# A two-layer hybrid decoder trunk: a root on ScalarE in the last norm, a decay table in two loads, keys copied by ScalarE, and the order of the first and last MLP groups

## The chip, the cores and the metric

One Trainium2 chip, one core of it. The time is device microseconds of one execution of the whole program: inputs in HBM, output in HBM. The median of three executions of the kernel before is 808.08 us (807.40 to 808.43).

## The reference

The input is 256 tokens of 1024 channels in float32. Two layers each do a mixer and an MLP, and a last RMSNorm follows. Cut to what the change touches:

```python
def rms_norm(x, g, eps=1e-6):
    return x * lax.rsqrt(jnp.mean(x * x, axis=-1, keepdims=True) + eps) * g

for l in range(2):
    h = rms_norm(x, attn_norm[l])
    p = h @ w_in[l]      # split into cq, ckv, k_rope, mq, mk, mv, rq, rk, rv, rg and three gates
    o_mla  = mla_branch(cq, ckv, k_rope, ...)       # norms of cq and ckv, up-projections, rope, causal softmax, 8 heads
    o_moba = moba_branch(mq, mk, mv, ...)           # causal softmax, 8 heads
    o_ret  = retention_branch(rq, rk, rv, rg, ...)  # rope, scores times a decay table, group norm, 4 heads
    merged = (sigmoid(g_mla) * (o_mla @ w_branch_mla) + sigmoid(g_moba) * (o_moba @ w_branch_moba)
              + sigmoid(g_ret) * (o_ret @ w_branch_ret))
    x = x + merged @ w_out[l]
    h = rms_norm(x, mlp_norm[l])
    x = x + jnp.square(jax.nn.relu(h @ w_up[l])) @ w_down[l]     # 1024 -> 4096 -> 1024
return rms_norm(x, final_norm)
```

## The kernel before, in words

**Precision.** Float32 products are made of three matmuls of split operands. A weight block arrives by DMA as `raw` (128x1024), ScalarE (ACT) rounds it to `whi` (L281), VectorE (DVE) subtracts to make `wlo` (L283), and `three` (L301) issues high by high, high by low and low by high into one PSUM bank (L302 to L304). Activations are split in the same way, as `xs` in the projections and as `sq` in the MLP's second product. In the projections whose output is wanted turned (`project_turned`, L506: keys and queries), the activations' two halves lie side by side, so that `acc` has two halves, and `join` (L493) adds them: ACT copies the second half (`second`), DVE adds it to the first (`qkraw`), and only then is the bank free for another product.

**Order of the work.** Each layer walks through units in this order: `b0` (the MLA's compressed columns c, and the first norm's sums), `mq`, `mk`, the MLA's up-projections `qrope`, `qnope` and `kvup`, `mv`, the gates, the retention's `rqk`, `rv` and `rg`, the branch products, `wout`, then the MLP in eight groups of 512 hidden columns. Steps that belong to no unit are hung into a slot of one with `at(slot(key, j), step)`. The order on each engine is then set by the tile framework's scheduler, except where the code pins it: `tc.keep_in_program_order`, `tc.issue_after`, and the table `behind`, which names for a weight block the instructions that its fetch, with its rounding, must come after (`have`, L203). Weight blocks are fetched in a fixed list, six pairs of rounded blocks deep.

**Copies of c (L819).** `c_copies` takes c out of PSUM in layer 1 and squares it; it is hung at the first unit of `mq`. `c_norms` follows a unit later.

**Keys of the MLA (L969, L1000).** `nope` copies the four 64x512 pieces of the keys out of PSUM into `KK`, and `kvup` calls it with DVE's copy; the same function copies the queries `Q` with ACT. The scores (L1039) read both.

**Retention tables (L1051).** `load_dec` loads one 1 MB table `dec` on SP's queue at the second unit of `rqk`. Its last 512 columns are the rope table, which DVE scales into `tab` (L526); its first 1536 are the decay, which the retention scores read (L1113). The rope multiplies `qkraw` and its swapped copy `qkoth` by parts of `tab` (L1097) and adds them (L1098); `swapped` (L531) makes `qkoth` with four DMAs on SP. `omlal` is the low half of the MLA's output.

**MLP (L1310 to L1372).** For each group, `squared_relu` takes two banks out with relu, squares them on ACT, and `turned_blocks` (L334) transposes them in 32x32 blocks on DVE, writes them to HBM (`bounce`) and reads them back in four DMAs (`hturned`), which turns them. `split_turned` rounds them to `sq` on ACT and subtracts on DVE (both L323). Some groups use a seven-product scheme in which sums of weight halves are made on DVE (`tsums`, `wsum`, L240) and rounded on ACT (`thi`, L233). In the last group, the weight fetches of the next blocks run on.

**Last norm (L1564 to L1587).** For each of two row tiles: ACT squares each of two 512-column banks with an accumulated sum (`fsq`, L1565), DVE adds the sums, POOL raises to the power -1/2 (L1580), DVE multiplies each bank by the gain out of PSUM (L1581), and the row factor is then applied by ACT to columns 0 to 319 and by DVE to the other 704 (L1583, L1586), each with its own output DMA.

Of the kernel before, what the change touches and what calls it, by code (L numbers as in the profile page):

```python
# [7 lines left out]
F32 = mybir.dt.float32  # L8
F32R = mybir.dt.float32r
BF16 = mybir.dt.bfloat16  # L10
AF = mybir.ActivationFunctionType
ALU = mybir.AluOpType
AX = mybir.AxisListType

P = 128
D = 1024
# [3 lines left out]
KD = D // P  # L20
DFF = 4096
NF = DFF // P
# [7 lines left out]
EPS = 1e-6  # L30
# [113 lines left out]
K_DEC = K_TURNED_MLA + 2 * S  # L144
K_TURNED_RT = K_DEC + RT_H * 3 * P
K_TURNED_MB = K_TURNED_RT + 2 * S
# [10 lines left out]
def trunk(ctx: ExitStack, tc: tile.TileContext, gx, wts, consts, gfin, gn, xtok, out):  # L157


    nc = tc.nc  # L160
# [4 lines left out]
    sb = ctx.enter_context(tc.tile_pool(name="sb", bufs=1))  # L165
# [10 lines left out]
    K = cp.tile([P, K_DEC], F32, name="K")  # L176
# [7 lines left out]
    neghalf = cp.tile([P, 8], F32, name="neghalf")  # L184
# [7 lines left out]
    order, loaded = list(where), {}  # L192
# [8 lines left out]
    behind = {}  # L201
# [110 lines left out]
    def small(name):  # L312
        return sb.tile([P, 8], F32, name=name, tag="st", bufs=SMALL)
# [20 lines left out]
    def turned_blocks(rows, name, tag, bufs, last=None, then=()):  # L334

        blocks = blocks_tile(name)
        for t in range(NT):
            turn = turn_row(blocks, t, rows[t])
        for key in then:
            behind.setdefault(key, []).append(turn)  # L340
        return turned_by_hbm(blocks, name, tag, bufs, last)
# [456 lines left out]
    def at(slot, step):  # L798
        steps.setdefault(slot, []).append(step)

    def slot(key, j):
        return [k for k, _ in prog].index((key, j))
# [9 lines left out]
    def layer(l, xn, before):  # L812

        c0 = []
        c, mla, mqkv, rqkv = {}, {}, {}, {}

        b0 = []

        def c_copies():  # L819

            for t in range(NT):
                ct = w2k("c0")
                m = small("ssc")
                c0.append((ct, m))
                nc.scalar.activation(ct[:, :416], b0[t][:, :416], AF.Copy)  # L825
                junk = sb.tile([P, 3 * P], F32, name="junk", tag="prob", bufs=4)
                for i, cs in enumerate((slice(0, MLA_QR), slice(MLA_QR, MLA_QR + MLA_KVR))):
                    n = cs.stop - cs.start
                    nc.scalar.activation(junk[:, :n], ct[:, cs], AF.Square, scale=n**-0.5, accum_out=m[:, i : i + 1])
# [98 lines left out]
        if l:  # L928
            project_turned(l, "mq", xn, moba_pair("mq"))
            for n in range(KD):  # L930
                at(slot("b0", 7), lambda n=n: xn.square(n))
            at(slot("mq", 0), c_copies)
            at(slot("mq", 1), c_norms)
            at(slot("mq", 2), xn.stats_row)
        else:
            mq = []
            for k in range(KD):
                prog.append((("start", k), lambda k=k: start(k, mq)))
            at(slot("start", KD - 2), lambda: xn.stats_rows(xrows))
            at(slot("start", KD - 1), c_copies)  # L940
            at(slot("start", KD - 1), c_norms)
            at(slot("start", KD - 1), xn.stats_row)
        project_turned(l, "mk", xn, moba_pair("mk"))
# [25 lines left out]
        def nope(dst, w, ks, copy, bank):  # L969
            for b in range(2):  # L970
                acc = bank("nope")
                for i in range(2):
                    cs = slice(P * (2 * b + i), P * (2 * b + i) + P)
                    for j, k in enumerate(ks):
                        three(
                            acc[:, S * i : S * i + S], w[0][:, j, cs], w[1][:, j, cs], c["h"][:, k, :], c["l"][:, k, :],
                            j == 0, j == len(ks) - 1,
                        )
                copy(dst[0:64, 4 * b : 4 * b + 4 : 2, :], halves(acc)[0:64])
                copy(dst[64:P, 4 * b + 1 : 4 * b + 4 : 2, :], halves(acc)[64:P])  # L980
# [18 lines left out]

        def kvup():  # L1000
            wh, wl = load_w(l, "kvup", 0)
            nope(mla["K"], (wh[:, :, 0:512], wl[:, :, 0:512]), (2,), nc.vector.tensor_copy, misc_tile)
            for t in range(NT):
                acc = misc_tile("pv")
                sl = slice(P * t, P * t + P)
                three(acc, c["h"][:, 2, sl], c["l"][:, 2, sl], wh[:, 0, 512:1024], wl[:, 0, 512:1024], True, True)
                nc.scalar.activation(mla["v"][t], acc, AF.Copy)
# [40 lines left out]

        th_moba = gates(l, "gmoba", xn)

        def load_dec():  # L1051

            rqkv["dec"] = sb.tile([P, K_TURNED_MB - K_DEC], F32, name="dec", tag="Q", bufs=1)
            tc.keep_in_program_order(nc.sync.dma_start(rqkv["dec"], consts[:, K_DEC:K_TURNED_MB]))

        merged, mT = {}, []
        if l == 0:
# [135 lines left out]
            tc.keep_in_program_order(nc.sync.dma_start(rg["gn"], src))  # L1193

        project(l, "rg", xn, 512, rg_done)
        at(slot("rqk", 1), load_dec)
        at(slot("rg", 2), load_gn)
        th_ret = gates(l, "gret", xn)
        order_out = ExitStack()
# [108 lines left out]
        us, h2, latest = {}, {}, []  # L1308
# [25 lines left out]
        def squared_relu(g):  # L1334

            rows = [w2k("relu") for _ in range(NT)]
            for t in range(NT):
                relu = nc.scalar.activation(rows[t], us[g][t], AF.Relu, scale=xm.col[t])
            for t in range(NT):
                nc.scalar.activation(rows[t], rows[t], AF.Square)  # L1340
            if g:
                waiting[g] = turned_blocks(rows, "h", "t4", T4)
            else:
                waiting[g] = turned_blocks(rows, "h", "t4", T4, (l, "down", 4, 0), [(l, "down", 2, 0)])
            if SEVEN[l][0] <= g - 2 < NF // 4 - 3:
                behind.setdefault(order[3 if g - 2 in SEVEN[l] else 4], []).append(relu)
            if 1 < g < NF // 4 - 1:
                h_ready(g - 1, relu)
            elif g != 1:
                h_ready(g)  # L1350
# [169 lines left out]
        if not last:  # L1520
            xn = Normed(G_ATT + KD * (l + 1), KD - 2)
            ys = {}


            have(ENDS[l])
            for j in range(ENDS[l], 4):
                behind[l + 1, "b0", j] = latest
            have(4)

            def copied(q):  # L1530
                ys[q] = w2k("ydn")
                copy = nc.vector.tensor_add(ys[q], accs[q], share[q])
                if q == 0:
                    tc.keep_in_program_order(copy)

            def turned(q):
                t, half = quarters[q]
                pt = misc_tile("pyd")
                for i in range(4):
                    nc.tensor.transpose(pt[:, P * i : P * i + P], ys[q][:, P * i : P * i + P], ident)  # L1540
                x_t = X[half][:, :, P * t : P * t + P]
                add = nc.vector.tensor_add(x_t, x_t, pt.rearrange("p (k s) -> p k s", k=4))
                if q == 0:
                    tc.keep_in_program_order(add)
                return xn.take_part(t, half)

            for q in range(4):
                ends[q]()
                copied(q)
                if q:  # L1550
                    turned(q - 1)

            def before(i):
                if i == 2:
                    behind[l + 1, "mq", 0, 0] = turned(3)
                if i == 7:
                    order_pe.close()

            return xn, before
# [7 lines left out]
        for t in range(NT):  # L1567
            y = sb.tile([P, D], F32, name="y", tag="t4", bufs=T4)
            r = sb.tile([P, 1], F32, name="fr", tag="st", bufs=SMALL)
            s0, s1, s2 = (st[:, 3 * t + i : 3 * t + i + 1] for i in range(3))  # L1570
            for half in range(2):
                cs = slice(512 * half, 512 * half + 512)
                ends[2 * t + half]()
                acc = accs[2 * t + half]
                if t == 0:
                    x_add(t, half)
                square(acc, 3 * t + half)
                if half:
                    nc.vector.scalar_tensor_tensor(s2, s0, EPS, s1, op0=ALU.add, op1=ALU.add)
                    nc.gpsimd.tensor_tensor(r, s2, neghalf[:, 0:1], op=ALU.pow)  # L1580
                nc.vector.tensor_mul(y[:, cs], acc, gf[:, cs])  # L1581
            cs = slice(0, 320)
            nc.scalar.activation(y[:, cs], y[:, cs], AF.Copy, scale=r)  # L1583
            nc.scalar.dma_start(out[:, t, cs], y[:, cs])
            cs = slice(320, D)
            nc.vector.tensor_scalar(y[:, cs], y[:, cs], r, None, op0=ALU.mult)  # L1586
            nc.sync.dma_start(out[:, t, cs], y[:, cs])  # L1587
        order_pe.close()
        return None, None

# [112 lines left out]
```

## Time and profile before

| what | value |
|---|---|
| median of three runs | 808.08 us |
| the profiled execution, and its span | 807.2 us, 805.4 us |
| granted TensorE clock, mean | 0.998 of 2.4 GHz |
| TensorE (PE) busy, matmuls | 797.0 us (99%), 3915 |
| DVE, ACT, POOL busy | 675.8 us, 483.1 us, 73.2 us |
| moved by DMA | 192.11 MB, 239 GB/s |
| chain that ended last | PE 89%, DMA 5%, DVE 3%, ACT 1% |

A span is from the first to the last instruction of the profiled execution; the execution's own time lies 1.8 us above it. Start times in rows count from the start of the span. In a timeline row the first number is the start, the second the duration in us (of the whole row where it stands for several, xN), then engine, line, operation, output and input; a bracket at the end gives the idle time before it and what ended it. PE is TensorE's matmul, SPq the DMA issue of the queue.

### The profile page before, as it was taken

How to read it: one execution, taken by the hardware profiler on the slowest of the kernel's cores; microseconds unless marked ns; L12 is line 12 of the kernel's file. 1: busy time of each engine (PE TensorE's matmuls, PEld its weight loads, DVE VectorE, ACT ScalarE, POOL GpSimd, SP SyncE). 2: the span in 40 equal slices, each digit the busy share in tenths (PEclk: the TensorE clock that was granted, in tenths of full speed). 3: DMA queues.
4: the chain of work that ended last, by engine and by line, in shares of the span. 5: the costliest groups of instructions: out<-in, count | busy, mean ns of one | idle time of the engine just before them, and what ended most of it. 6: DMA issues, size and time to landing. Idle time of an engine off the chain costs nothing.

```text
span 805.4 us, 11403 instructions
## 1 busy us (share of the span) xinstructions
PE 797.0 (99%) x3915; PEld 665.1 (83%) x3915; DVE 675.8 (84%) x1136; ACT 483.1 (60%) x747; POOL 73.2 (9%) x63
## 2 busy tenths in 40 slices
PE   9999999999999999999999999999999999999996
PEld 7888887888888888888788888888888878888885
DVE  6769997978888898887797987699698878899786
ACT  7775654653557666666486566655545666667562
POOL 0100810000030000000025220000000300000000
PEclk9999999999999999999999999999999999999999
DMA  9975889975678677778656579688665687788741
GB/s 335 338 244 179 281 241 297 282 235 173 222 225 244 228 255 248 252 269 259 209 163 228 157 232 326 213 261 273 217 223 192 186 272 260 241 280 319 261 169 54
DMA packets 68122, 192.11 MB, mean 239 GB/s; under 512 B 8288, under 2 KB 25056, under 8 KB 67808
## 3 DMA queue, kind: packets, MB, share of 16 engines
q1 hardware_dynamic: 67488, 190.71, 72.4%
q8 instruction: 31, 0.51, 0.3%
q10 hardware_dynamic: 576, 0.67, 0.2%
q14 instruction: 27, 0.22, 0.1%
HBM read 168.81 MB, written 18.87 MB: 233 GB/s over the span
## 4 chain that ended last, share of the span: by engine, by line
PE 89%; DMA 5%; DVE 3%; ACT 1%; SPq 1%; issue 1%; DVEq 0%; ACTq 0%
PE acc L302 16%; PE acc L304 16%; PE acc L303 16%; PE pup L302 6%; PE pup L304 6%; PE pup L303 6%; PE acc L1273 6%; PE acc L515 4%; PE acc L517 2%; DMA raw<-wts 2%; DMA hturned<-bounce 2%; DMA bounce<-hblocks 1%; PE ps_s L1039 1%; PE acc L881 1%; DMA qkoth<-qkraw 1%; DVE wlo L283 1%
## 5 line engine op out<-in xcount | busy, mean ns | idle before, releaser
L281 ACT ACTIVATE whi<-raw 128x1024 fp32r<-128x1024 f32 (+3 forms) x263 | 264.8, 1019 | 170.5 <-PE acc L304 98.1
L283 DVE TENSOR_TENSOR wlo<-raw,whi 128x1024 fp32r<-128x1024 f32 (+3 forms) x263 | 313.8, 1209 | 48.9 <-ACT whi L281 46.1
L302 PE MATMUL acc<-whi,xs 128*128 128x512 f32 (+1 forms) x304 | 119.4, 394 | 0.2
L303 PE MATMUL acc<-wlo,xs 128*128 128x512 f32 (+1 forms) x304 | 117.8, 388 | 0.0
L304 PE MATMUL acc<-whi,xs 128*128 128x512 f32 (+1 forms) x304 | 117.7, 388 | 0.0
L303 PE MATMUL pup<-wlo,xs 128*128 128x512 f32 x256 | 99.8, 390 | 0.0
L304 PE MATMUL pup<-whi,xs 128*128 128x512 f32 x256 | 99.6, 389 | 0.0
L302 PE MATMUL pup<-whi,xs 128*128 128x512 f32 x256 | 99.4, 389 | 0.0
L304 PE MATMUL acc<-whi,sq 128*128 128x512 f32 x184 | 72.0, 391 | 0.7 <-DVE sq L323 0.5
L302 PE MATMUL acc<-whi,sq 128*128 128x512 f32 x184 | 71.8, 390 | 0.0
L303 PE MATMUL acc<-wlo,sq 128*128 128x512 f32 x184 | 71.6, 389 | 0.0
L302 PEld LDWEIGHTS acc<-whi,xs 128*128 128x128 f32 x304 | 57.0, 188 | 13.6 <-issue 0.8
L304 PEld LDWEIGHTS acc<-whi,xs 128*128 128x128 f32 x304 | 57.1, 188 | 11.3
L303 PEld LDWEIGHTS acc<-wlo,xs 128*128 128x128 f32 x304 | 57.1, 188 | 10.7
L304 PEld LDWEIGHTS pup<-whi,xs 128*128 128x128 f32 x256 | 48.1, 188 | 9.9
L303 PEld LDWEIGHTS pup<-wlo,xs 128*128 128x128 f32 x256 | 48.1, 188 | 9.8
L302 PEld LDWEIGHTS pup<-whi,xs 128*128 128x128 f32 x256 | 47.9, 188 | 9.8
L606 ACT ACTIVATE prob<-prob,smx 128x128 f32<-128x128 f32 x64 | 28.3, 444 | 31.5 <-DVE smx L603 31.5
L391 POOL TENSOR_TENSOR sqsum<-sqsum,xsq 128x256 f32<-128x256 f32 x16 | 18.2, 1140 | 310.8 <-ACT xs L318 165.5
L304 PEld LDWEIGHTS acc<-whi,sq 128*128 128x128 f32 x184 | 34.5, 188 | 9.2 <-DVE sq L323 2.0
L323 DVE TENSOR_TENSOR sq<-hturned,sq 128x1024 fp32r<-128x1024 f32 x16 | 19.6, 1224 | 25.9 <-ACT sq L323 21.7
L515 PE MATMUL acc<-xs,whi 128*128 128x512 f32 x160 | 40.7, 395 | 0.4 <-ACT c L825 0.4
(275 smaller groups left out, 1398.7 us busy)
## 6 DMA issues: line engine op xcount, KB each, us to landing
raw<-wts SPq DMA_DIRECT2D x264, 512.0 KB, 4.9
bounce<-hblocks SPq DMA_DIRECT2D x16, 512.0 KB, 3.6
hturned<-bounce SPq DMA_DIRECT2D x64, 128.0 KB, 3.2
pbounce<-blocks SPq DMA_DIRECT2D x8, 768.0 KB, 4.0
probT<-pbounce SPq DMA_DIRECT2D x32, 192.0 KB, 5.9
qkoth<-qkraw SPq DMA_DIRECT2D x48, 64.0 KB, 4.8
raw<-wts SPq DMA_DIRECT2D x5, 464.0 KB, 6.1
dec<-consts SPq DMA_DIRECT2D x2, 1024.0 KB, 7.1
```

The lines of the kernel that those rows point to most:

```text
L281: fetched.append(nc.scalar.activation(hi[:, cs], raw[:, cs], AF.Copy))
L283: nc.vector.tensor_sub(lo[:, cs], raw[:, cs], hi[:, cs].bitcast(F32))
L302: nc.tensor.matmul(o, ah, bh, start=start, stop=False, **more)
L303: nc.tensor.matmul(o, ah, bl, start=False, stop=False, **more)
L304: nc.tensor.matmul(o, al, bh, start=False, stop=stop, **more)
L323: return nc.scalar.activation(hi, src, AF.Copy), nc.vector.tensor_sub(lo, src, hi.bitcast(F32))
L391: (nc.gpsimd if n < self.on_pool else nc.vector).tensor_add(self.sum, self.sum, sq)
L515: nc.tensor.matmul(acc, wh[:, k, :], xn.both(k), start=k == 0, stop=False)
L517: nc.tensor.matmul(acc[:, 0:S], wl[:, k, :], xn.k(k)[0], start=False, stop=k == KD - 1)
L606: nc.scalar.activation(p[:, a:b], p[:, a:b], AF.Exp, bias=m[:, 2 + i : 3 + i], scale=d**-0.5, accum_out=m[:, 4 + i : 5 + i])
L881: nc.tensor.matmul(mq[n], wq[n][0], xn.both(k), start=k == 0, stop=False)
L1273: nc.tensor.matmul(o, a, b, start=half == 0 and i == 0, stop=4 * half + n == KD and i == len(jobs) - 1)
```

## The change

Five parts, in the order of the diff.

1. `c_copies` in layer 1 moves to the last unit of `b0` and is split from the squares, which stay at `mq`.
2. `kvup` copies the keys with ACT.
3. The table is loaded in two parts: `load_tab` (512 columns, at the first unit of `rqk`) and `load_dec` (1536 columns, at the fourth unit of `rv`).
4. In the MLP, the first group pins one `up` fetch behind its read-back and two `down` fetches behind its transposes; the last group pins two fetches behind its squares, and in layer 0 one `b0` block of the next layer behind its read-back.
5. The last norm takes a root on ACT, of the one sum with the other (and epsilon) as bias, and a reciprocal on DVE; the last bank is scaled by factor and gain in one operation out of PSUM, and ACT scales the first 512 columns.

```diff
             for t in range(NT):
                 ct = w2k("c0")
-                m = small("ssc")
-                c0.append((ct, m))
+                c0.append((ct, small("ssc")))
                 nc.scalar.activation(ct[:, :416], b0[t][:, :416], AF.Copy)
+
+        def c_squares():
+
+            for ct, m in c0:
...
-            at(slot("mq", 0), c_copies)
+            at(slot("b0", 7), c_copies)
+            at(slot("mq", 0), c_squares)
...
-            nope(mla["K"], (wh[:, :, 0:512], wl[:, :, 0:512]), (2,), nc.vector.tensor_copy, misc_tile)
+            nope(mla["K"], (wh[:, :, 0:512], wl[:, :, 0:512]), (2,), nc.scalar.copy, misc_tile)
...
+        def load_tab():
+
+            dec = rqkv["dec"] = sb.tile([P, K_TURNED_MB - K_DEC], F32, name="dec", tag="Q", bufs=1)
+            src = consts[:, K_TURNED_RT:K_TURNED_MB]
+            tc.keep_in_program_order(nc.sync.dma_start(dec[:, K_TURNED_RT - K_DEC :], src))
+
         def load_dec():
 
-            rqkv["dec"] = sb.tile([P, K_TURNED_MB - K_DEC], F32, name="dec", tag="Q", bufs=1)
-            tc.keep_in_program_order(nc.sync.dma_start(rqkv["dec"], consts[:, K_DEC:K_TURNED_MB]))
+            cs = slice(0, K_TURNED_RT - K_DEC)
+            tc.keep_in_program_order(nc.sync.dma_start(rqkv["dec"][:, cs], consts[:, K_DEC:K_TURNED_RT]))
...
-        at(slot("rqk", 1), load_dec)
+        at(slot("rqk", 0), load_tab)
+        at(slot("rv", 3), load_dec)
...
             for t in range(NT):
-                nc.scalar.activation(rows[t], rows[t], AF.Square)
+                squared = nc.scalar.activation(rows[t], rows[t], AF.Square)
+            if g == NF // 4 - 1:
+                for key in order[1:3]:
+                    behind.setdefault(key, []).append(squared)
             if g:
-                waiting[g] = turned_blocks(rows, "h", "t4", T4)
+                waiting[g] = turned_blocks(rows, "h", "t4", T4, None if last or g < NF // 4 - 1 else (l + 1, "b0", 2))
             else:
-                waiting[g] = turned_blocks(rows, "h", "t4", T4, (l, "down", 4, 0), [(l, "down", 2, 0)])
+                waiting[g] = turned_blocks(rows, "h", "t4", T4, (l, "up", 3, 1), [(l, "down", i, 0) for i in (2, 3)])
...
-                if half:
-                    nc.vector.scalar_tensor_tensor(s2, s0, EPS, s1, op0=ALU.add, op1=ALU.add)
-                    nc.gpsimd.tensor_tensor(r, s2, neghalf[:, 0:1], op=ALU.pow)
-                nc.vector.tensor_mul(y[:, cs], acc, gf[:, cs])
-            cs = slice(0, 320)
+                if half == 0:
+                    nc.vector.tensor_scalar(s2, s0, EPS, None, op0=ALU.add)
+                    nc.vector.tensor_mul(y[:, cs], acc, gf[:, cs])
+            nc.scalar.activation(s1, s1, AF.Sqrt, bias=s2)
+            nc.vector.reciprocal(r, s1)
+            nc.vector.scalar_tensor_tensor(y[:, cs], acc, r, gf[:, cs], op0=ALU.mult, op1=ALU.mult)
+            nc.sync.dma_start(out[:, t, cs], y[:, cs])
+            cs = slice(0, 512)
             nc.scalar.activation(y[:, cs], y[:, cs], AF.Copy, scale=r)
             nc.scalar.dma_start(out[:, t, cs], y[:, cs])
-            cs = slice(320, D)
-            nc.vector.tensor_scalar(y[:, cs], y[:, cs], r, None, op0=ALU.mult)
-            nc.sync.dma_start(out[:, t, cs], y[:, cs])
```

How the order of instructions moves, at three places. First, DVE in layer 0 from the first join of `rqk` on, before (the row of L526 is the scaled rope table, L620 are transposes of MLA probabilities):

```order
L497 TENSOR_TENSOR qkraw<-acc,second 128x256
L283 TENSOR_TENSOR wlo<-raw,whi 128x1024
L497 TENSOR_TENSOR qkraw<-acc,second 128x256
L283 TENSOR_TENSOR wlo<-raw,whi 128x1024
L497 TENSOR_TENSOR qkraw<-acc,second 128x256
L283 TENSOR_TENSOR wlo<-raw,whi 128x1024
L497 TENSOR_TENSOR qkraw<-acc,second 128x256
L620 STREAM_TRANSPOSE blocks<-prob 128x3x4x32 x2
L283 TENSOR_TENSOR wlo<-raw,whi 128x1024
L526 TENSOR_TENSOR tab<-dec,rrow 128x512
L1097 TENSOR_TENSOR qkT<-qkraw,tab 128x512
L1097 TENSOR_TENSOR qkoth<-qkoth,tab 128x512
```

The same place in the changed kernel (L1108 is what was L1097):

```order
L497 TENSOR_TENSOR qkraw<-acc,second 128x256
L283 TENSOR_TENSOR wlo<-raw,whi 128x1024
L526 TENSOR_TENSOR tab<-dec,rrow 128x512
L497 TENSOR_TENSOR qkraw<-acc,second 128x256
L283 TENSOR_TENSOR wlo<-raw,whi 128x1024
L1108 TENSOR_TENSOR qkT<-qkraw,tab 128x512
L497 TENSOR_TENSOR qkraw<-acc,second 128x256
L283 TENSOR_TENSOR wlo<-raw,whi 128x1024
L497 TENSOR_TENSOR qkraw<-acc,second 128x256
L620 STREAM_TRANSPOSE blocks<-prob 128x3x4x32 x2
L1108 TENSOR_TENSOR qkoth<-qkoth,tab 128x512
L1108 TENSOR_TENSOR qkT<-qkraw,tab 128x512
```

The table now stands between the first and the second join, and the first product with it between the second and the third.

Second, ACT in the first MLP group of layer 1, before (L1338 is the relu, L1340 its square, `thi` the rounded weight sums):

```order
L281 ACTIVATE whi_6506<-raw_6504 128x1024
L1338 ACTIVATE relu_6393<-pup_6312,ms_6352 128x512
L1338 ACTIVATE relu_6394<-pup_6313,ms_6352 128x512
L233 ACTIVATE thi_6608<-tsums_6604 128x1024
L1340 ACTIVATE relu_6393<-relu_6393 128x512
L1340 ACTIVATE relu_6394<-relu_6394 128x512
L281 ACTIVATE whi_6524<-raw_6522 128x1024
L281 ACTIVATE whi_6544<-raw_6542 128x1024
```

and in the changed kernel:

```order
L281 ACTIVATE whi_6508<-raw_6506 128x1024
L1350 ACTIVATE relu_6395<-pup_6314,ms_6354 128x512
L1350 ACTIVATE relu_6396<-pup_6315,ms_6354 128x512
L1352 ACTIVATE relu_6395<-relu_6395 128x512
L1352 ACTIVATE relu_6396<-relu_6396 128x512
L281 ACTIVATE whi_6526<-raw_6524 128x1024
L281 ACTIVATE whi_6546<-raw_6544 128x1024
L233 ACTIVATE thi_6610<-tsums_6606 128x1024
L281 ACTIVATE whi_6564<-raw_6562 128x1024
L323 ACTIVATE sq_6411<-hturned_6406 128x1024
```

The squares follow the relus directly, and the rounded sums come two weight blocks later.

Third, ACT at the end of the changed kernel (L1580 squares with a sum, L1596 is the root, L1601 the scaling):

```order
L1580 ACTIVATE fsq_7786,fst_7753<-acc_6311 128x512
L1596 ACT_TABLE_LOAD
L1596 ACTIVATE fst_7753<-fst_7753 128x1
L1601 ACTIVATE y_7754<-y_7754,fr_7755 128x512
L1580 ACTIVATE fsq_7808,fst_7753<-acc_6312 128x512
L1602 DMA y<-y_7754 128x512
L1580 ACTIVATE fsq_7824,fst_7753<-acc_6313 128x512
L1596 ACTIVATE fst_7753<-fst_7753 128x1
L1601 ACTIVATE y_7794<-y_7794,fr_7795 128x512
```

One table load stands ahead of the first row tile's root, and none ahead of the second's.

## Rows read from the trace of the kernel before

**Rows 1.** The page, busy time, share of the span and instructions of each engine:

```profile
PE 797.0 (99%) x3915; PEld 665.1 (83%) x3915; DVE 675.8 (84%) x1136; ACT 483.1 (60%) x747; POOL 73.2 (9%) x63
```

**Rows 2.** What TensorE waited for: us in total, times, longest:

```profile
PE acc L304 <- DVE sq L323: 0.5, 1, 0.5
PE acc L515 <- ACT c L825: 0.4, 1, 0.4
PE ps_s L1039 <- DVE KK L980: 0.2, 1, 0.2
```

**Rows 3.** Timeline of layer 1's first MLP group, ACT, DVE and PE:

```profile
640.36 1.24 ACT L1338 ACTIVATE relu<-pup,ms 128x512 f32<-128x512 f32 x2
...
642.76 1.14 ACT L1340 ACTIVATE relu<-relu 128x512 f32<-128x512 f32 x2
...
644.03 1.30 DVE L332 STREAM_TRANSPOSE hblocks<-relu 128x512 f32<-128x512 f32 x2
...
655.40 1.23 DVE L323 TENSOR_TENSOR sq<-hturned,sq 128x1024 fp32r<-128x1024 f32 x1 [0.55 <-ACT sq L323]
...
655.77 0.39 PE L303 MATMUL acc<-wlo,sq 128*128 128x512 f32 x1
...
656.68 0.50 PE L304 MATMUL acc<-whi,sq 128*128 128x512 f32 x1 [0.52 <-DVE sq L323]
```

**Rows 4.** Timeline, TensorE in layer 0's first and last MLP group:

```profile
257.54 0.39 PE L303 MATMUL acc<-wlo,sq 128*128 128x512 f32 x1
...
258.05 0.50 PE L304 MATMUL acc<-whi,sq 128*128 128x512 f32 x1
...
389.89 0.39 PE L303 MATMUL acc<-wlo,sq 128*128 128x512 f32 x1
...
390.38 0.50 PE L304 MATMUL acc<-whi,sq 128*128 128x512 f32 x1
```

**Rows 5.** Timeline of layer 0 around the joins and the table, PE, SP's queue, DVE:

```profile
118.10 0.39 PE L304 MATMUL acc<-whi,xs 128*128 128x512 f32 x1
...
118.58 0.50 PE L302 MATMUL acc<-whi,xs 128*128 128x512 f32 x1
...
118.63 2.42 SPq L537 DMA_DIRECT2D qkoth<-qkraw  x4
...
121.04 0.42 DVE L497 TENSOR_TENSOR qkraw<-acc,second 128x256 f32<-128x256 f32 x1
...
128.06 0.69 DVE L526 TENSOR_TENSOR tab<-dec,rrow 128x512 f32<-128x512 f32 x1 [4.55 <-DMA dec<-consts]
...
133.85 0.39 PE L304 MATMUL acc<-whi,xs 128*128 128x512 f32 x1
...
134.34 0.50 PE L302 MATMUL acc<-whi,xs 128*128 128x512 f32 x1
```

**Rows 6.** The swapped copies' tile, its DMAs, both layers:

```profile
DMA to landing us min/median/max: 2.0/4.2/8.4
```

**Rows 7.** Timeline of the last norm, ACT and DVE:

```profile
799.40 0.60 ACT L1565 ACTIVATE fsq<-acc 128x512 f32<-128x512 f32 x1 [2.02 <-PE acc L304]
799.89 0.19 ACT L1565 ACTIVATION_READ_ACCUMULATOR fsq<-acc 128x1 f32 x1
...
800.99 0.59 DVE L1586 TENSOR_SCALAR y<-y,fr 128x704 f32<-128x704 f32 x1
```

**Rows 8.** Groups by line: engine, operation, count | busy us, mean ns | idle before:

```profile
L1581 DVE TENSOR_TENSOR y<-acc,gf 128x512 f32<-128x512 f32 x4 | 2.7, 684 | 0.5 <-ACT fsq L1565 0.5
...
L980 ACT COPY Q<-nope 64x512 f32<-64x512 f32 x4 | 2.3, 582 | 0.0
...
L789 ACT ACT_TABLE_LOAD x1 | 1.3, 1283 | 1.7 <-PEq L1696 1.7
```

**Rows 9.** Stretches: length, PE, PEld, DVE, ACT, POOL busy, PEclk, DMA share, GB/s:

```profile
62.00:75.00 13.00, 13.00 (x63) 11.01 (x62) 12.87 (x43) 9.22 (x23) 0.00 (x0) 1.00 0.53 163
118.00:135.00 17.00, 16.81 (x102) 12.62 (x101) 12.41 (x25) 4.63 (x7) 0.00 (x0) 1.00 0.94 313
```

More of the change, by code (lines that the diff above doesn't have):

```diff
@@ L940, in layer @@
             at(slot("start", KD - 1), c_copies)
+            at(slot("start", KD - 1), c_squares)
             at(slot("start", KD - 1), c_norms)
@@ L1526, in layer @@
             for j in range(ENDS[l], 4):
-                behind[l + 1, "b0", j] = latest
+                behind.setdefault((l + 1, "b0", j), []).extend(latest)
             have(4)
```

## The prediction

> **What bounds the kernel now.** I read the page first: TensorE is busy 797.0 us of a span of 805.4 [rows 1]. The reader should take two things from that row. No engine but TensorE can set the time of the middle, and nothing in this change takes a matmul away, so all that can be won is the 8.4 us in which TensorE does not run: its few waits, and the stretch after its last matmul. The second view is therefore the list of what TensorE waited for: three entries that the change touches, 0.5, 0.4 and 0.2 us [rows 2]. Those idle times are too small as prices, because a matmul shows 0.39 us busy but the next starts 0.23 us after it. So the third view is the timeline of TensorE around each wait, where the loss is the start-to-start distance less 0.23. In the first MLP group of layer 1 it is 656.68 - 655.77 - 0.23 = 0.68 [rows 3], while the idle time there reads 0.52: a listed wait costs its idle time and some 0.16 more. Read so, two waits appear that the list leaves out, 258.05 - 257.54 - 0.23 = 0.28 and 390.38 - 389.89 - 0.23 = 0.26 [rows 4], and two more in the retention projections of layer 0, 0.25 at 118.58 and 0.26 at 134.34 [rows 5]. The last view is the timeline after the last matmul [rows 7].
>
> **The change part by part.**
>
> *First MLP group, both layers.* Before, ACT squared the group at 642.76, after a weight sum's rounding that stood between it and the relus, which had ended at 640.36 + 1.24 = 641.60; DVE transposed it from 644.03 on, and DVE's low half of the squares ended at 655.40 + 1.23 = 656.63, where TensorE took it at 656.68 and had been ready at 655.77 + 0.23 = 656.00 [rows 3]. Now the squares stand right behind the relus, the transposes ahead of the weight sums, and the four reads of the bounce right behind its write on SP. The squares end 1.2 us earlier; the transposes, no longer behind the rounding's low half, start at about 642.2, 1.9 us earlier. The need is 0.63 us earlier, and so with the transfers as long as before both losses go: 0.68 and 0.28. What is late next on ACT is the second group's relu, behind the squares of the first; it is off TensorE's path by about the time the squares come forward. The weight fetch that stood between the bounce's write and its reads now stands behind the reads; the six pairs of rounded weights in hand carry its lateness.
>
> *Last MLP group of layer 0.* Squares now stand ahead of the next weight block's rounding on ACT, a 128x1024 operation that takes longer than the 0.26 us needed. That loss goes. Layer 1's last group shows no loss and gives nothing.
>
> *Copies of c (layer 1).* They leave the head of the second query unit, where TensorE waited 0.4 for them [rows 2], for the places right behind their projection. Gain 0.4 + 0.16, say 0.55. The rounding of weights queued behind them is late by at most two copies and runs blocks ahead.
>
> *Keys copied by ScalarE.* TensorE's wait for the last copy on DVE, 0.2 + 0.16 = 0.4 with rounding [rows 2], goes, as the copies no longer stand behind a low half and the query rope on DVE. ACT takes four copies of 0.58 = 2.3 us a layer [rows 8]. In layer 0, where TensorE waits for no key, I cost it at nothing: ACT is busy 9.22 of 13 us right after [rows 9], and this idle time hides it. Without that cover the first softmax there is late by 0.7, about one copy.
>
> *Table in two loads.* In layer 0, DVE lay idle 4.55 us at 128.06 for the one large load, then made the scaled rope table in 0.69 [rows 5]. Now the small load comes first, and the 0.69 us operation stands ahead of the second join, the one that empties the bank for which TensorE already waits 0.25 at 118.58. Its cost there is between nothing (if the join's other part, on ACT, ends last anyway) and 1.4 (0.69, and the 0.7 of lateness above); I take 0.6, the operation itself less its overlap, as DVE shows no other room. The wait at 134.34 is for the low halves of the MLA output. The fourth join ends at 121.04 + 0.42 + 0.6 = 122.1, four swap transfers take 2.4 to issue [rows 5] and 4.2 to land [rows 6], so about 128.7; behind them DVE has four operations of 0.69 and a low half of 1.23 [rows 3, 5], to 132.7. TensorE needs them at 134.08 + 0.6 = 134.7. So 0.26 goes. With the longest landing, 8.4 [rows 6], the end is 136.9, and 2.2 is lost. The second table load issues later than the old one and is read only by the scores much further on. Layer 1 shows no loss at either place, and I give it nothing.
>
> *Last norm.* The last sum is read at 799.89 + 0.19 = 800.08, and the last scaling ended at 800.99 + 0.59 = 801.58 [rows 7]. POOL's power and DVE's 704 columns go. Now: a root of 128x1 on ACT, which no row shows; the bounds are the 0.19 of a 128x1 read [rows 7] and the 0.58 of a wide copy [rows 8], and I take 0.2, the nearer shape. Then a reciprocal of 128x1, by the same read 0.19, and one DVE pass over 512 PSUM columns, 0.68 as the multiplication that it replaces [rows 8]. With 0.05 for each hand-over the three end at 800.33, 800.57 and 801.30: 0.28 gained, with bounds 0.29 and -0.10. A root needs another function table on ACT: the one load of the trace took 1283 ns [rows 8]. The new order has one more load, in the chain of the first row tile. There it puts 1.28 of load, 0.2 and 0.19 in place of the 0.9 us that lie between the last read and the last scaling [rows 7], and scales 512 columns; about 1 us more in all. ACT lay idle 2.02 us before the last square [rows 7], which hides it with 1 us over.
>
> **Sum.** 0.68 + 0.28 + 0.26 + 0.55 + 0.40 + 0.28 = 2.45 gained, less 0.6 and plus 0.26 in layer 0: 2.1. The profiled execution took 807.2, so 805.1; the median of the runs is 808.08, 0.88 above it, and by that 806.0. What a measurement of this kernel can tell from no change is 0.2%, 1.6 us.
>
> **The rivals.**
>
> A. *Layer 0 takes it back.* ACT's four copies do delay the roundings of layer 0, and DVE behind them: 2.3 of copies, about 1.2 for a low half that now goes ahead of the transposes there, and 0.6 for the table would make 4.1 at the second join in place of 0.6. I price it at half of the difference, 1.8: 807.8; in full it is 809.5. For it: DVE is busy 12.87 of 13 us from 62 on [rows 9], so what is put ahead of the join has nowhere to go. Against it: ACT's idle 3.8 us there, in which the copies fall.
>
> B. *The chains start earlier but land no earlier.* The change does not do what it says: the bounce and its reads meet the weight fetches, and the squares arrive as before. Then 0.68 + 0.28 + 0.26 = 1.2 is not won: 807.2. For it: 11 us lie between the transposes at 644.03 and the low half at 655.40 [rows 3], nearly all in transfers. Against it: the reads are now ahead of fetches on SP.
>
> C. *Slower: DVE waits for the swaps instead of the table.* The swapped halves of the retention queries and keys now stand on DVE ahead of the MLA output's low halves with no table load to wait for first, so a late landing is not covered any more. It decides from a landing of 4.2 + 2.0 = 6.2 us on. At 8.4 layer 0 loses the 0.26 that I count as won and 2.2 more, and layer 1, where the same order stands and I reckon with the same room, another 2.2: 4.7, so 810.7. For it: the DMA engines are busy 0.94 of the stretch from 118 to 135 [rows 9]. Against it: 8.4 is the longest of all such landings, and it would have to come in both layers.
>
> D. *The table switch costs more than its row.* If the switch costs a second time its 1.28 [rows 8], the 1 us that is left before the last square is overdrawn by 0.3: 806.3. No row shows such an extra: against it. The Trainium skill, page "ScalarE: Activation LUTs", section "What ACT_TABLE_LOAD costs", states about 1283 ns for the load and about 1380 ns more for draining the engine, some 2.66 us for every switch to another set of functions. The load's figure agrees with the row; by the whole figure, the overdraft would be an estimated 0.4 and the time 806.4, and no run here shows the drain.
>
> **How the numbers follow.** Forecast 0.57, A 0.18, B 0.12, D 0.05, C 0.08. Faster by over 0.2% (under 806.5): the forecast and D, 0.62. Within: A and B, 0.30. Slower by over 0.2% (above 809.7): C, 0.08. The range begins where layer 0 loses nothing and both its waits go, 2.45 + 0.25 + 0.26 = 3.0, with a little for a shorter last transfer: 804.9; it ends past A and B at 808.1, and leaves C out.
>
> **What would show it.** In the changed kernel's profile: TensorE's list without the squares, c and the key; matmuls 0.23 apart in the first groups; the layer 0 join's loss at 0.8 to 0.9; no idle DVE before the rope table; the last DVE pass ending 1.2 us after the last sum is read, instead of 1.5. The prediction is wrong if TensorE's losses in layer 0 between 64 and 136 us grow by more than 1 us, if the squares' low half ends as late as before against the group's start, or if a second table load stands behind the last square.

## The result, and the profile after

The changed kernel is slower: 813.50 us, median of 6 runs, against 807.74 for 6 runs of the kernel before; the ratio is 1.0076, with a 95% interval of 1.0061 to 1.0091. The forecast was 806.0. The profiled execution took 812.54, its span is 810.7 against 805.4.

TensorE has the same work in the same busy time; the 5.3 us by which the span grew are nearly all time in which it does not run. The page's first row, and the whole list of what TensorE waited for in the changed kernel:

```profile
PE 797.1 (98%) x3915; PEld 665.7 (82%) x3915; DVE 671.6 (83%) x1128; ACT 489.5 (60%) x758; POOL 73.1 (9%) x61
```

```profile
PE pup L302 <- DVE carried L1426: 6.4, 4, 3.4
PE warm L792 <- PEq L1711: 0.8, 1, 0.8
PE acc L515 <- ACT th L712: 0.4, 1, 0.4
PE acc L302 <- DVE qkraw L497: 0.2, 1, 0.2
```

The three entries of before [rows 2], the squares, c and the key, are gone, as forecast. One that the forecast does not know has come: the third MLP group's up product waits 6.4 us in all, in both layers, for `carried`, two DVE copies that empty the banks it writes to (L1411 before, L1426 now, in `seven`).

The chain that leads there, in layer 0. Timeline of the kernel before: on ACT the relu of the second group and the rounding of the first group's squares, on SP the bounce of the second group, on ACT the third group's relu and the rounding of the second group's squares, on DVE the first copy, and TensorE's product that needs it:

```profile
251.40 1.37 ACT L1338 ACTIVATE relu<-pup,ms 128x512 f32<-128x512 f32 x2 [0.98 <-PE pup L304]
...
255.67 1.06 ACT L323 ACTIVATE sq<-hturned 128x1024 fp32r<-128x1024 f32 x1 [0.40 <-DMA hturned<-bounce]
...
256.66 0.33 SPq L346 DMA_DIRECT2D bounce<-hblocks  x1
...
265.42 1.37 ACT L1338 ACTIVATE relu<-pup,ms 128x512 f32<-128x512 f32 x2 [0.98 <-PE pup L304]
...
267.73 1.06 ACT L323 ACTIVATE sq<-hturned 128x1024 fp32r<-128x1024 f32 x1 [0.93 <-DMA hturned<-bounce]
...
271.69 0.68 DVE L1411 COPY carried<-pup 128x512 f32<-128x512 f32 x1
...
273.38 0.39 PE L302 MATMUL pup<-whi,xs 128*128 128x512 f32 x1
```

The same in the changed kernel, with the first group's rounding ahead of it:

```profile
253.01 1.06 ACT L323 ACTIVATE sq<-hturned 128x1024 fp32r<-128x1024 f32 x1 [3.04 <-DMA hturned<-bounce]
253.98 1.25 ACT L1350 ACTIVATE relu<-pup,ms 128x512 f32<-128x512 f32 x2
...
259.40 0.33 SPq L346 DMA_DIRECT2D bounce<-hblocks  x1
...
264.54 1.37 ACT L1350 ACTIVATE relu<-pup,ms 128x512 f32<-128x512 f32 x2 [0.98 <-PE pup L304]
...
271.40 1.06 ACT L323 ACTIVATE sq<-hturned 128x1024 fp32r<-128x1024 f32 x1 [5.49 <-DMA hturned<-bounce]
...
272.28 0.39 PE L304 MATMUL acc<-whi,sq 128*128 128x512 f32 x1
...
272.50 1.23 DVE L323 TENSOR_TENSOR sq<-hturned,sq 128x1024 fp32r<-128x1024 f32 x1 [7.67 <-ACT sq L323]
...
275.37 0.68 DVE L1426 COPY carried<-pup 128x512 f32<-128x512 f32 x1
...
276.11 0.50 PE L302 MATMUL pup<-whi,xs 128*128 128x512 f32 x1 [3.44 <-DVE carried L1426]
...
277.30 0.80 PE L302 MATMUL pup<-whi,xs 128*128 128x512 f32 x1 [0.23 <-DVE carried L1426]
...
278.32 0.63 PE L304 MATMUL pup<-whi,xs 128*128 128x512 f32 x1
...
278.75 0.63 PE L302 MATMUL pup<-whi,xs 128*128 128x512 f32 x1
```

What the reader is to see: ACT sits 3.04 us at the first group's rounding, whose data has not landed, and the second group's relu stands behind it and starts 2.6 us later than before. The bounce starts 2.7 us later, the second group's own rounding 3.7. TensorE itself runs ahead of before here: the third group's relu, which follows it directly, starts 0.9 us earlier (264.54 against 265.42), so against TensorE the second group's rounding is 4.6 us later: it starts 6.86 us behind that relu, where it was 2.31. Now DVE sits 7.67 us at its subtraction while the two copies that TensorE needs stand behind it in DVE's queue. Their input had been complete since about 269. TensorE had started the product at 273.38 before; its turn came at 272.28 + 0.23 = 272.51 now, and it ran at 276.11.

The granted clock shows a second price. Stretches of the changed kernel, columns as in [rows 9]:

```profile
272.00:276.20 4.20, 0.76 (x4) 0.30 (x3) 3.70 (x5) 4.20 (x6) 0.00 (x0) 1.00 0.05 19
276.20:280.60 4.40, 4.17 (x11) 3.04 (x12) 4.40 (x7) 1.09 (x2) 0.00 (x0) 0.61 0.70 238
...
674.00:678.50 4.50, 1.78 (x7) 0.88 (x6) 4.50 (x8) 4.21 (x5) 0.00 (x0) 1.00 0.22 43
678.50:690.00 11.50, 11.50 (x52) 9.47 (x52) 11.50 (x15) 6.24 (x7) 0.00 (x0) 1.00 0.80 266
```

After 3.4 us of idle the clock granted to TensorE is 0.61 in the mean of the next 4.4 us: most of them at the lower level, 1.2 of 2.4 GHz, with matmuls 0.43 apart (278.32, the next at 278.75) instead of 0.23. In layer 1 the wait is 2.49 and the clock stays at 1.00. Added up by start-to-start distances less 0.23, layer 0 loses 3.6 to the wait and 1.9 to what follows it, layer 1 loses 3.05: 8.6 us. Of the 1.9, 0.4 is a second wait, for the other bank's copy (at 277.30; layer 1 has the same 0.4 within its 3.05), so the lower clock takes 1.5.

The last norm, the changed kernel's timeline, the first row tile's table load and root and then the second row tile:

```profile
800.83 0.19 ACT L1580 ACTIVATION_READ_ACCUMULATOR fsq<-acc 128x1 f32 x1
...
801.04 1.28 ACT L1596 ACT_TABLE_LOAD   x1
...
802.34 0.30 ACT L1596 ACTIVATE fst<-fst 128x1 f32<-128x1 f32 x1
...
805.53 0.19 ACT L1580 ACTIVATION_READ_ACCUMULATOR fsq<-acc 128x1 f32 x1
...
805.76 0.29 ACT L1596 ACTIVATE fst<-fst 128x1 f32<-128x1 f32 x1
806.09 0.16 DVE L1597 RECIPROCAL fr<-fst 128x1 f32<-128x1 f32 x1 [1.14 <-ACT fst L1596]
806.29 0.72 ACT L1601 ACTIVATE y<-y,fr 128x512 f32<-128x512 f32 x1 [0.23 <-DVE fr L1597]
806.29 0.75 DVE L1598 SCALAR_TENSOR_TENSOR y<-acc,fr,gf 128x512 f32<-128x512 f32 x1
```

From the end of the second row tile's read (805.53 + 0.19 = 805.72) to the end of the last DVE pass (807.04) it is 1.32 us; before it was 1.50 [rows 7].

### The profile page after: what moved, and what is told of

It is laid out like the page before. It is cut to its first block, busy times and chain, and to the rows that moved or that the text cites. A ratio compares the mean times of both kernels' runs of the same rounds, so it can differ in the third digit from the quotient of the medians.

```text
span 810.7 us, 11402 instructions
## 1 busy us (share of the span) xinstructions
PE 797.1 (98%) x3915; PEld 665.7 (82%) x3915; DVE 671.6 (83%) x1128; ACT 489.5 (60%) x758; POOL 73.1 (9%) x61
## 4 chain that ended last, share of the span: by engine, by line
PE 93%; DMA 2%; DVE 2%; ACT 1%; issue 1%; SPq 0%; DVEq 0%; ACTq 0%
PE acc L302 16%; PE acc L304 16%; PE acc L303 16%; PE pup L302 7%; PE pup L304 7%; PE pup L303 7%; PE acc L1285 6%; PE acc L515 4%; PE acc L517 2%; PE ps_s L1044 1%; DMA bounce<-hblocks 1%; DMA hturned<-bounce 1%; PE acc L884 1%; PE po L678 1%; PE ps_s L584 1%
```

## The experiments

The theory after the first look: ACT's and DVE's queues are in order, and the new order puts a rounding that waits for a transfer ahead of work that is ready (ACT), and the same a step later on DVE. The rival: the moved weight fetches collide with the second group's transfers, whatever the order on ACT. A third: another of the five parts costs too. The ratios below are against runs of the kernel before on the same chip. e1 to e4 share a chip, and so do e5 to e8, and e9 and e10.

**e1, the relu first.** In the changed kernel:

```diff
-            if 1 < g < NF // 4 - 1:
+            if 0 < g < NF // 4 - 1:
                 h_ready(g - 1, relu)
-            elif g != 1:
+            elif g:
                 h_ready(g)
```

> The changed kernel, but in the first MLP group the rounding of the squares (ACT, sq from hturned) may only be issued after the relu of the second group; all pins of weight fetches stay. Theory 1 (ACT's order): the new order puts sq of group 0, which waits for its transfer, ahead of the relu of group 1; ACT sits at it (3.04 us in layer 0, 3.43 in layer 1), the relu, squares, transposes and bounce of group 1 come 2.7 us later, its own sq lands 3.7 us later, and on DVE the copies of the two banks that group 2's up products need (carried) stand behind it. The trace loses some 5.5 us in layer 0 (3.4 of wait, then matmuls at the lower clock for 3 us) and 3.05 us in layer 1. So this edit gives 813.5 - 8.6 = about 805, with no TensorE wait for carried over 0.5 us. Theory 2 (transfers): the moved weight fetches collide with the second group's bounce and read-back, which take 1.3 us longer; the order on ACT is incidental. Then the wait stays above 1.5 us in each layer and the time stays above 810.

Measured: 806.43 us, 0.9985 (0.9971 to 0.9999); the profiled execution 805.53. TensorE's wait for `carried` in the profile:

```profile
PE pup L302 <- DVE carried L1426: 0.8, 1, 0.8
```

All pins stand, and 6.4 us have become 0.8, in layer 0 alone. What the rival forecast, a wait above 1.5 and a time above 810, did not come. The expectation was off in two things: 0.8 is above the 0.5 that I allowed, and the median is 1.4 above 805, with runs from 804.7 to 808.4. Nor does the run show that the relu's place on ACT is the cause. Timeline in layer 0, ACT's relu of the third group and the rounding of the second, then DVE:

```profile
265.51 1.37 ACT L1350 ACTIVATE relu<-pup,ms 128x512 f32<-128x512 f32 x2 [0.98 <-PE pup L304]
...
272.08 1.06 ACT L323 ACTIVATE sq<-hturned 128x1024 fp32r<-128x1024 f32 x1 [3.22 <-DMA hturned<-bounce]
...
270.22 0.65 DVE L1426 COPY carried<-pup 128x512 f32<-128x512 f32 x1
273.18 1.23 DVE L323 TENSOR_TENSOR sq<-hturned,sq 128x1024 fp32r<-128x1024 f32 x1 [2.31 <-ACT sq L323]
274.32 0.69 DVE L1426 COPY carried<-pup 128x512 f32<-128x512 f32 x1
```

The second group's relu is back in its place, and still that group's rounding starts 272.08 - 265.51 = 6.57 us behind the third group's relu, where it was 6.86 in the changed kernel and 2.31 before. What let TensorE go on is an order that the edit moved without naming it: the first of the two copies now stands ahead of the late subtraction on DVE. The second still stands behind it, and that is the 0.8. The transfers have their share of the lateness: from the issue of the bounce to the rounding, in layer 0, it is 11.07 us before, 12.00 in the changed kernel and 12.93 here, where the bounce is issued at 259.15.

**e2, the first group's pins as before**, the other four parts as changed:

```diff
-                waiting[g] = turned_blocks(rows, "h", "t4", T4, (l, "up", 3, 1), [(l, "down", i, 0) for i in (2, 3)])
+                waiting[g] = turned_blocks(rows, "h", "t4", T4, (l, "down", 4, 0), [(l, "down", 2, 0)])
```

> The changed kernel with the first MLP group's pins as before (last on the down block 4, the transposes ahead of down block 2 only); the other four parts stay. Theory 1 and theory 2 both put the whole loss on these pins: 813.5 - 8.6 + 0.96 (the two small waits of the first group come back) = about 806, faster than before by the copies of c 0.5, the keys 0.4, the last group 0.26 and the tail 0.2 to 0.3. Theory 3 (another part also costs, for instance the four key copies on ACT make ACT late in the MLP): above 808.

Measured: 805.82 us, 0.9971 (0.9958 to 0.9984). As theory 1 and the rival both had it; the third theory falls. The rest of the change is worth 0.3%. The kernels on this chip that keep the new pins without the large wait, e1 and e4, are not faster than this one (806.43 and 806.88): the 0.96 us that the pins save in the trace does not show in the times.

**e3, those pins alone**, the reverse edit in the kernel before.

> The kernel before with nothing but the first MLP group's new pins. Theory 1 and 2: 807.7 + 8.6 - 0.96 = about 815.4, with TensorE waiting for carried in both layers. Theory 3: clearly less than that, under 811.

Measured: 816.66 us (4 runs), 1.0105 (1.0082 to 1.0128). The loss stands without the other parts, and is 1.3 larger than expected. In its profiled execution, the longest of the four, the clock fell in both layers; the stretch after the wait of layer 0, and that of layer 1:

```profile
276.60:282.00 5.40, 5.39 (x13) 4.16 (x14) 5.40 (x9) 1.20 (x2) 0.00 (x0) 0.50 0.54 195
...
681.50:688.00 6.50, 6.50 (x22) 4.74 (x21) 6.50 (x11) 1.87 (x2) 0.00 (x0) 0.74 0.65 220
```

A granted clock of 0.50 is the lower of the two levels for the whole stretch, 0.74 for about half of it.

**e4, one of the two pins**, the transposes' (`then`), with the read-back's (`last`) as before:

```diff
-                waiting[g] = turned_blocks(rows, "h", "t4", T4, (l, "up", 3, 1), [(l, "down", i, 0) for i in (2, 3)])
+                waiting[g] = turned_blocks(rows, "h", "t4", T4, (l, "down", 4, 0), [(l, "down", i, 0) for i in (2, 3)])
```

> The changed kernel with the new pins of the two down blocks behind the transposes, but the read-back pinned ahead of down block 4 as before. In this order the squares stand right behind the relus, and sq of group 0 stands behind the relu of group 1 and one of its squares. Theory 1: no wait of TensorE for carried, about 805 to 806. Theory 2 (the pin of the fetches behind the read-back does the harm): also about 805 to 806, as that pin is the old one. It tells whether one of the two pins alone gives the gain of the first group.

Measured: 806.88 us, 0.9987 (0.9971 to 1.0003); the profiled execution 805.25, without the first group's waits and with 0.2 for `carried`. So this pin alone brings the squares forward. Of the kernels here, the first group's rounding goes ahead of the second's relu only in those with both pins; the read-back's pin alone was not tried. The second group's rounding is late here too, 271.72 - 265.70 = 6.02 us behind the third group's relu, and one copy stands ahead of its subtraction.

**e5, the copies first.** The first group's rounding stays ahead of the relu. Instead the second group's rounding is held behind the third group's squares on ACT, and its subtraction behind the two copies on DVE:

```diff
-            if 1 < g < NF // 4 - 1:
+            if g == 2:
+                late[:] = [squared]
+            elif 1 < g < NF // 4 - 1:
                 h_ready(g - 1, relu)
...
-        waiting = {}
+        waiting, late = {}, []
...
+            if late and first:
+                with tc.issue_after(emptied[-1].ins):
+                    h_ready(1, late.pop())
             if final:
                 shares()
```

> The changed kernel, with sq of group 0 still ahead of the relu of group 1 on ACT, but with sq of group 1 issued behind group 2's squares on ACT and behind the two copies of the banks (carried) on DVE. Theory 1 in full (two in-order stands): ACT still holds the second group back by 2.6 us, but the copies no longer stand behind the late squares on DVE, and TensorE never waits for carried: about 805. If the lateness of the second group reached TensorE in another way too, by its squares themselves, a new wait of TensorE for sq of over 1 us would show in each layer and the time would be above 808.

Measured: 803.82 us, 0.9958 (0.9944 to 0.9972), without any wait for `carried` or `sq`, in 5 runs from 803.65 to 804.59. Its timeline in layer 0, ACT and DVE:

```profile
253.73 1.06 ACT L323 ACTIVATE sq<-hturned 128x1024 fp32r<-128x1024 f32 x1 [2.70 <-DMA hturned<-bounce]
254.69 1.25 ACT L1350 ACTIVATE relu<-pup,ms 128x512 f32<-128x512 f32 x2
...
270.32 1.25 DVE L1428 COPY carried<-pup 128x512 f32<-128x512 f32 x2
272.29 1.23 DVE L323 TENSOR_TENSOR sq<-hturned,sq 128x1024 fp32r<-128x1024 f32 x1 [0.72 <-ACT sq L323]
```

ACT still sits 2.7 us and the relu is as late as in the changed kernel, yet TensorE waits for none of it, with both copies ahead of the subtraction: the lateness reached TensorE only through the place of the copies in DVE's queue.

**e6, both orders**: e1 and e5 together (`late[:] = [relu]`).

> Both edits together: sq of group 0 behind the relu of group 1 (as in the first run) and sq of group 1 behind the copies of the banks. Theory 1: the 0.8 us wait for carried that the first run kept in layer 0 goes too: about 0.9 us under the first run's profiled 805.5, and since no idle stretch of TensorE is left there, the runs should scatter less than the first run's 804.7 to 808.4. If the scatter stays, it has another source.

Measured: 803.80 us, 0.9961 (0.9949 to 0.9974), 5 runs from 803.64 to 804.57. The wait for `carried` is gone, 1.1 under e1's profiled execution, and the runs lie closer together, as expected; on the same chip e7, which keeps e1's order, ran from 804.75 to 808.59. With the relu in its place the second group's rounding is as late as ever, 272.46 - 265.46 = 7.00 us behind the third group's relu. e5 does as well: of the two mends the one on DVE is the one that counts.

**e7, one table load**, on e1's kernel, with `load_dec` of before at its place of before.

> The first run's kernel with the decay table in one load as before. The prediction's price: the table's 0.6 us at the second join goes, and the 0.26 us at the MLA's low halves comes back: 0.35 faster. By the traces so far the join's loss went from 0.25 to 0.38 only: then about 0.13 gained and 0.26 lost, no difference that can be measured.

Measured: 805.90 us, 0.9986 (0.9977 to 0.9995). The join's loss went from 0.39 to 0.24 in the trace. Not conclusive as a time: the wait for `carried`, 1.0 us, had moved into layer 1 in that execution, and hides what is asked. At the low halves of the MLA output this trace loses nothing.

**e8, the last norm alone**, in the kernel before.

> The kernel before with the new last norm alone. From the last read of the sum to the end of the last DVE scaling: 1.50 before; the prediction said 1.22, the changed kernel's trace shows 1.32. If the part stands by itself: 1.32 again, one table load of 1.28 ahead of the first row tile, and nothing else moved.

Measured: 807.09 us in one run. From the end of the read to the end of the last pass 1.31; ACT's idle time ahead of the last square fell from 2.02 [rows 7] to 0.88. By the trace the part stands by itself; one run, on a chip on which the kernel before took 806.96, shows no gain in time. The other small losses moved although their code is the same: the first group of layer 0 loses 0.61 where it lost 0.28, the low halves 0.37 where they lost 0.26. Differences of 0.1 to 0.3 us at such places, between two single traces, are within that.

**e9, layer 0's keys on DVE**, on e6's kernel:

```diff
-            nope(mla["K"], (wh[:, :, 0:512], wl[:, :, 0:512]), (2,), nc.scalar.copy, misc_tile)
+            nope(mla["K"], (wh[:, :, 0:512], wl[:, :, 0:512]), (2,), nc.scalar.copy if l else nc.vector.tensor_copy, misc_tile)
```

> The kernel with both orders mended, its layer 0 keys copied by DVE as before (layer 1 stays on ACT). It asks where layer 0 gives back 0.68 us at 112 (TensorE waits for ACT's th, which starts 0.73 later than before against TensorE) and 0.39 at 119. If the key copies on ACT make layer 0's softmax late: the wait at 112 falls under 0.3, 0.4 to 0.7 us gained in the trace. If the swaps' new order on SP and POOL's later work on DVE's port do it: the wait stays near 0.6.

Measured: 803.56 us (4 runs, 803.16 to 803.66), 0.9947 (0.9929 to 0.9966): faster than both kernels, and the lowest median of all, though its interval overlaps with those of e5 and e6 on another chip. The whole list of what TensorE waited for:

```profile
PE warm L792 <- PEq L1716: 0.8, 1, 0.8
```

The wait at 112 (0.68) is gone and so is that at 119 (0.39). But the edit also moved the second batch of swaps behind two weight fetches on SP again, and POOL's work on them back behind a pause of 4.87 us; the six low halves that DVE makes beside it took 11.24 us instead of 12.86. Whether ACT's copies or POOL's earlier work made layer 0 late stays open.

**e10, one table load** on e6's kernel.

> The kernel with both orders mended, its decay table in one load as before. By the run with one load on the other base: the loss at 119 goes from 0.39 to 0.24, a loss at the MLA's low halves of up to 0.27 returns or stays away, and the wait at 112 stays at 0.55 to 0.68. No difference over 0.3 us in the trace, and none that can be measured in the runs.

Measured: 805.56 us, 0.9974 (0.9965 to 0.9984). The expectation was wrong. TensorE's list, and DVE at the table:

```profile
PE acc L302 <- DVE omlal L323: 0.8, 2, 0.6
...
PE acc L515 <- ACT th L712: 0.5, 1, 0.5
```

```profile
129.92 0.69 DVE L526 TENSOR_TENSOR tab<-dec,rrow 128x512 f32<-128x512 f32 x1 [5.61 <-DMA dec<-consts]
```

The join's loss went from 0.39 to 0.25, but DVE sat 5.61 us for the one load, and TensorE lost 0.74 and 0.40 at the low halves of the MLA output, which e6 does not lose: by these two traces the loads are worth 1.0 us, not a tie; the two ratios, 0.9974 and e6's 0.9961, differ by as much, within their intervals. On e1's base the same edit lost nothing at the low halves, and the ratios are alike (e7 0.9986, e1 0.9985), so the size is open.

## Why the prediction was wrong

By its own steps:

- **The first MLP group, the step that failed.** The small waits of both layers went, as worked out. What failed is the sentence on what is late next: "the second group's relu, behind the squares of the first; it is off TensorE's path by about the time the squares come forward." The working set against the relu's lateness how much earlier the data of the rounding ahead of it would land, and not how long ACT would sit there. In the trace of before the relu started at 251.40 in layer 0 and that data were taken at 255.67: of these 4.3 us, 1.9 were to be won, so ACT had to sit for some 2.4 with the relu behind it; it sat so that the relu came 2.6 late. And "off TensorE's path" was not followed past ACT, to the copies of the banks, which stand on DVE behind the second group's subtraction. The kernel before had just 1 us there (272.37 to 273.38), and the second group came 4.6 later. Cost: 3.6 + 1.9 in layer 0, 3.05 in layer 1, in place of a gain of 0.96 alone. e2 and e3 show that these pins bring the loss, e5 that it reaches TensorE by the place of the copies on DVE. Why the second group is late is shown in part only: with the relu in its place, in e1, e4 and e6, its rounding is 6.0 to 7.0 us behind the third group's relu all the same. How much of that is the bounce, which is issued later, and how much the transfers, which take longer, was not tried and stays open.
- **Last group of layer 0, copies of c, keys in layer 1.** Right: by start-to-start distances TensorE loses nothing at these places after. Priced 0.26, 0.55 and 0.40.
- **Keys in layer 0, costed at nothing.** Not borne out: TensorE lost 0.55 us there at 111, waiting for `th`, where it had lost nothing listed; e9 gains it back, by one of two ways.
- **The table.** Right in kind, the sizes off: the join's loss grew from 0.25 to 0.38, not to 0.85; the 0.26 at the low halves went. No trace with two loads loses anything there; with one load the traces lose 0 (e7) to 1.1 us (e10). So the part is worth between a loss of 0.15 (e7 against e1) and a gain of 1.0 (e10 against e6), where I had a loss of 0.35.
- **The last norm.** 0.18 gained, in place of 0.28: the root took 0.29, where I took 0.2, and the pass 0.75, where I took the multiplication's 0.68. The table load took 1.28 and fell in the first row tile's chain, as worked out. Rival D fell: the root starts 802.34 - 801.04 = 1.30 after the load does. What the page "ScalarE: Activation LUTs" of the Trainium skill adds for a drain (section "What ACT_TABLE_LOAD costs") does not show behind the load here, nor ahead of it: it starts 0.02 after the read's end (800.83 + 0.19 = 801.02).
- **The rivals.** The slower side came, and by none of them: A looked at layer 0's joins, C at the swaps there, and B had the first group's squares land no earlier and said nothing of the second group. None of the signs named for being wrong came either: TensorE's losses in layer 0 between 64 and 136 us grew by 0.4 (0.55 + 0.38 against 0.25 + 0.26). They watched places that had been priced already.
- **The rest of the sum.** Without the wait for `carried` the parts come to 0.68 + 0.28 + 0.26 + 0.55 + 0.40 + 0.18 + 0.26 - 0.13 - 0.55 = 1.9 by the traces, where I had 2.1. The times are lower than that: 813.5 - 8.6 = 804.9, where I had 806.0, and e5 and e6 measured 803.8, on a chip on which the kernel before took 806.96. About 1 us of it is not accounted for.

## What to carry to other kernels

When an edit moves an instruction that waits for a transfer ahead of others on an in-order engine, put the landing time, as the trace has it, against the time at which the first instruction behind it is ready; the difference is lateness, whatever the transfer gained. Then follow it until it ends: through each queue in which the late result is waited for, asking what ready work stands behind it there; here it was two copies that only freed a bank. The list of waits does not show a stage with 1 us of room: here 4.6 us of lateness used it up. And when an edit that mends one order takes the wait away, look in its trace whether the lateness went too: in e1 it stayed, and another order had moved.

## What the runs showed of the hardware

In the changed kernel an idle stretch of TensorE of 3.44 us was followed by matmuls at the lower of the two clock levels, which cost 1.5 us more; one of 2.49 cost nothing more. In e3 a stretch of 3.25 cost 2.8 more, and one of 2.91 cost 1.4, the clock falling only some 1.2 us after TensorE had started again. These are single executions: the longer stretch did not cost the more. The kernels in which TensorE still waits at some place scatter over 2 to 5 us (e1 804.7 to 808.4, e4 805.1 to 810.3, e7 804.8 to 808.6, e10 804.4 to 807.0); the kernel before ran from 805.5 to 811.9 on the chip of e1 to e4 and from 805.9 to 808.3 on that of e5 to e8. e5, e6 and e9 lie within 1 us each, e5 and e6 though they keep 0.65 and 0.68 us at 112 and 0.4 at 119. That the waits behind the MLP's transfers, and the table's, make the scatter is a likely reading from few runs; it was not tried by itself. The multiplication of a PSUM bank by a row factor and a gain in one DVE operation took 0.75 us, the multiplication by the gain alone 0.68.
